# A hybrid decoder trunk with 32 experts: first-block picks with the slot matrix stationary, 8 KB of DMA scratch and an eleventh weight slot

## The chip, the cores and the metric

The kernel runs on one core of a Trainium2 chip. The metric is the device time of one execution in microseconds (us); lower is better. TensorE (PE; its weight loads are listed apart, as PEld), VectorE (DVE), ScalarE (ACT), GpSimd (POOL) and SyncE (SP) are the engines. SP issues the loads of weights; ACT issues a few transfers on a queue of its own, and POOL issues software DMAs, the indirect gathers among them.

## What is computed

One layer over 512 tokens of width 1024: a mixer of four branches with gates and an output projection `w_out`, then a mixture of experts. All is float32. The part that the change touches begins at `w_out`:

```python
x = x + g1 * hybrid_mixer(h, ..., w_out)             # ... merged @ w_out
h = rms_norm(x, norm2_g) * (1.0 + sc2) + sh2
x = x + g2 * hier_moe(h, ...)
# hier_moe, per token: top 1 of 4 groups, top 2 of its 8 experts, gate = group prob * softmax of the two
# expert e, on the tokens routed to it:
y = (silu(xe @ w1[e]) * (xe @ w3[e])) @ w2[e]        # w1, w3: 1024 x 512, w2: 512 x 1024
out = segment_sum(y * gate)
```

## The kernel before

The mixer (up to about 740 us) is the same in both kernels. After it come three stages.

**`w_out`, in two halves.** The 512 tokens are four tiles of 128; half 0 has tiles 0 and 1, half 1 has tiles 2 and 3. Each half makes four products of 256 columns (`mm<-wh,mh` and the like: 48 matmuls of three high and low terms). A result is scaled into one of two buffers `yo` by VectorE, added to `xm`, squared on ScalarE, transposed (`z`), evacuated as `xT` by ScalarE, and multiplied by the router's weights (`pl`, the logits). Half 1 uses the two weight blocks that half 0 used last, then loads and splits (`wh` on ScalarE, `wl` on VectorE) the first two again.

**Routing** (`route`, once for each half). The rows of the half, divided by their norm, are written to the DRAM tensor `xhd`: tile `t` is scaled by ScalarE into a buffer and sent by ScalarE's queue. In both halves the first tile goes through `xg[0]` (1024 columns), the second through the two `yo` buffers (512 columns each). VectorE works through a long chain of small operations (first maxima `f0`, `f1`, `f2`, one-hot rows `oe` and `ohb`); TensorE counts with `ohb` into `pl`, which gives each token's slot `rank` at its expert; `orr` is the one-hot matrix of slots. `tb` and `tg` are products with it that give each slot its token (`toki`, `tok`) and gate (`gx`, `ga`).

**Experts, two at a time.** Block `p` (0 to 15) holds experts 2p and 2p+1 with 64 slots each. `turn_in(p)` transposes the gathered rows `xg[p % 2]` and scales them to `xe`; `front` multiplies by `w1` and `w3` (`ph`, tile `g`); `Back` transposes `g`, multiplies by `w2` (`py`) and spreads the result over the tokens (`po`). The rows come from `fetch(p)`, an indirect DMA from `xhd`. Block 0 isn't fetched: its rows are picked out of `xm` by products with the first slots' one-hot matrix `rp` (in `g1b`), with `xm` as the stationary operand, eight column groups `d` by four token tiles. That gives the transposed rows at once, in `pt0`. The picks for tiles 0 and 1 stand between the routing's steps (`meanwhile`), those for tiles 2 and 3 behind `rank`. `fetch(1)` and `fetch(2)` are issued ahead of the loop, `fetch(p + 2)` in `turn_in(p)`.

**The ring of weights.** `order` lists 198 loads (186 of 1 MB, 12 of 0.5 MB), in the order in which the blocks use them. SP issues them in that order, each into the next slot of a ring of 20: `EWX` slots of the pool `ewx`, six of the freed weight pool `wst`, and four that held `mh` and `ml`, put in at the places `RL`. A load waits until its slot is free. The first `EWX` loads are issued inside half 1 of `w_out`.

TensorE's instructions run in the order of the code from here on (`manual_schedule`), VectorE's too while half 1 is routed; ScalarE's and POOL's order is the scheduler's.

Of the kernel before, what the change touches and what calls it, by code (L numbers as in the profile page):

```python
# [9 lines left out]
F32 = mybir.dt.float32  # L10
# [5 lines left out]
AF = mybir.ActivationFunctionType  # L16
# [5 lines left out]
D = 1024  # L22
KD = D // 128
NT = S // 128
# [1 line left out]
O_CV, O_SB, O_RT = 2048, 3072, 4608  # L26
TAPS = (0, 0, 1, 3, 2)
W = dict(h0=15, h1=3, h2=8, l0=7, l1=4, f0=15, sk=11, sq=7, s1=2, s2=5, s3=1, s4=5, s5=0.5, s6=3, t0=4, c0=8, c1=6, c2=9, r=5, ce=20)
EWX = 10
RL = (10, 11, 18, 19)  # L30
WS = (10, 3, 6, 6, 12)
LATE = 4
WARM = (1, 0, 0, 2)
# [4 lines left out]
def trunk(ctx, tc, x, c, ada_w, ada_b, norm1_g, norm2_g, w_in, hgrn_lb, hgrn_norm_g, conv_w, conv_b, conv_ln_g,  # L38
          conv_ln_b, sb_qnorm_g, sb_knorm_g, ret_norm_g, w_branch, w_gate, b_gate, w_out, router_group_w,
          router_group_b, router_expert_w, router_expert_b, expert_w1, expert_w3, expert_w2, out):  # L40
    nc = tc.nc
    V, A, P, T = nc.vector, nc.scalar, nc.gpsimd, nc.tensor
# [14 lines left out]
    def mm(o, l, r, start, stop):  # L57
        T.matmul(o, l, r, start=start, stop=stop, skip_group_check=True)  # L58
# [12 lines left out]
    def psm(nm="mm"):  # L71
        return ps_mm.tile([128, 512], F32, name=nm, tag="mm")

    def psz(nm="z2"):
        return ps_z.tile([128, 2, 512], F32, name=nm, tag="z2")
# [194 lines left out]
    a = A.activation(wh[:, 4:], raw[:, 4:], AF.Copy)  # L270
# [85 lines left out]
    def three(o, l, r, nk, first=True, last=True):  # L356

        (lh, ll), (rh, rl) = l, r
        for k in range(nk):
            pace()  # L360
            mm(o, lh(k), rh(k), first and k == 0, False)
            mm(o, lh(k), rl(k), False, False)
            mm(o, ll(k), rh(k), False, last and k == nk - 1)
# [597 lines left out]
    xm = keep.tile([128, NT, D], F32, name="xm")  # L961
# [44 lines left out]
    nr = nrm.enter_context(tc.tile_pool(name="nr", bufs=1))  # L1006
    yo = [nr.tile([128, 2, 256], F32, name="yo", bufs=2) for _ in range(2)]
# [26 lines left out]
    xg = [kp.tile([128, D], F32, name="xg0")]  # L1034
# [14 lines left out]

    ewx = ctx.enter_context(tc.tile_pool(name="ewx", bufs=EWX, side="right"))  # L1050
    order = []
# [14 lines left out]
    for p in range(16):  # L1066
# [5 lines left out]
        for ks, cs in cuts(p):  # L1072
            for e in es:
                order.append(four(expert_w2[0][e])[:, ks, cs])
    ring = [(ewx, "ew")] * EWX + [(wst, tag) for tag in ("raw", "raw", "wh", "wh", "wl", "wl")]
    for r, tag in zip(RL, ("ml", "mh", "ml", "mh")):
        ring[r:r] = [(late, tag)]
# [16 lines left out]
    def first_max(v, n, nm, hot=True):  # L1094

        iob = io[:, None, :n].to_broadcast([128, 2, n])
        bc = lambda a: a[:, :, None].to_broadcast([128, 2, n])
        mx = nr.tile([128, 2], F32, name=nm + "m", bufs=2)
        V.reduce_max(mx, v, axis=AX.X)
        tmp = nr.tile([128, 2, n], F32, name=nm + "t", bufs=2)  # L1100
        V.tensor_tensor(tmp, v, bc(mx), op=OP.is_lt)
        V.scalar_tensor_tensor(tmp, tmp, 64.0, iob, op0=OP.mult, op1=OP.add)
        idx = nr.tile([128, 2], F32, name=nm + "i", bufs=2)
        V.tensor_reduce(idx, tmp, axis=AX.X, op=OP.min)
        oh = None
        if hot:
            oh = nr.tile([128, 2, n], F32, name=nm + "o", bufs=2)
            V.tensor_tensor(oh, iob, bc(idx), op=OP.is_equal)
        return mx, idx, oh

    def pick(ts, ds):

        for d in ds:
            a, k = divmod(d, 4)
            for t in ts:
                mm(pt0[:, d], xm[:, t, a * 512 + k:(a + 1) * 512:4], rp[t // 2][:, t % 2], t == 0 and k == 0, t == NT - 1)

    def meanwhile():


        scr = psm("scr")
        for n, ds in zip(WARM, ((), range(4), range(4, 8), ())):
            for _ in range(n):
                mm(scr, ident, xm[:, 0, :512], True, True)
            pick((0, 1), ds)
            a = yield
            if a is not None:
                mm(scr[:a.shape[-1], :2], a, ident[:, :2], True, True)
        yield

    def fetch(p):

        P.indirect_dma_start(out=xg[p % 2], out_offset=None, in_=xhd[:, :],  # L1133
                             in_offset=bass.IndirectOffsetOnAxis(ap=toki[:, p:p + 1], axis=0),
                             bounds_check=S - 1, oob_is_err=False)
# [3 lines left out]
    oR, ev, gv, cr, rp, pt0 = [], [], [], [], [], None  # L1139

    def route(half, pl, between=None):

        then = between or (lambda a: None)
        ts = slice(2 * half, 2 * half + 2)
# [6 lines left out]
            V.scalar_tensor_tensor(lg[:, i], pl[:, i * 36:(i + 1) * 36], r[:, i:i + 1], crow, op0=OP.mult, op1=OP.add)  # L1151
        for i in range(2):
            t = 2 * half + i
            for cs, xs in ((slice(0, D), xg[0]),) if not i else ((slice(0, 512), yo[0]), (slice(512, D), yo[1])):
                if i:
                    xs = xs.rearrange("p a b -> p (a b)")
                A.activation(xs, xm[:, t, cs], AF.Copy, scale=r[:, i:i + 1])
                nc.scalar.dma_start(xhd[t * 128:(t + 1) * 128, cs], xs)
        gm, gi, og = first_max(lg[:, :, :4], 4, "f0")
# [13 lines left out]
        v2, i2, _ = first_max(eg, 8, "f2", False)  # L1173
# [10 lines left out]
        for i in range(2):  # L1184
            t = 2 * half + i
# [17 lines left out]
        if half:  # L1203
            tb = psm("tb")
            by_slot(tb[:, :16], lambda h, k_, i, j: ev[h][:, k_, i, j::2])
            slots0(1)
            pick((2, 3), range(8))
            V.tensor_scalar(toki, tb[:, :16], 1024.0, None, op0=OP.add)
            V.tensor_scalar(tok, tb[:, :16], 1024.0, None, op0=OP.add)

# [35 lines left out]
    def by_slot(o, what, first=True):  # L1246

        n = 0
        for h in range(2):
            for k_ in range(2):  # L1250
                for i in range(2):
                    for j in range(2):
                        mm(o[64 * j:64 * j + 64], oR[h][:, k_, i], what(h, k_, i, j), first and n == 0, n == 7)
                    n += 1
# [18 lines left out]
    for half in range(2):  # L1273
        pl = ps_o.tile([128, 512], F32, name="pl", tag="o1")
        ts = slice(2 * half, 2 * half + 2)
        cbs = (0, 1, 2, 3) if half == 0 else (2, 3, 0, 1)
        for n, cb in enumerate(cbs):
            if half == 0 or cb < 2:
                wo[cb] = wblock(w_out, 0, KD, cb * 256, 256)
            w = wo[cb]  # L1280
            if half and n == 3:
                load_to(EWX)
            cs = slice(cb * 256, cb * 256 + 256)
            o = psm()
            for i in range(2):
                three(o[:, i * 256:(i + 1) * 256],
                      tuple((lambda k, a=a: a[:, k, i * 128:(i + 1) * 128]) for a in (mh[half], ml[half])),
                      tuple((lambda k, a=a: a[:, k, :]) for a in w), KD, first=i == 0)
            y = yo[n % 2]
            V.tensor_mul(y, o.rearrange("p (t c) -> p t c", t=2), g1b[:, None, cs].to_broadcast([128, 2, 256]))  # L1290
            (V if half else P).tensor_add(xm[:, ts, cs], xm[:, ts, cs], y)
            for i in range(2):
                A.activation(y[:, i], xm[:, 2 * half + i, cs], AF.Square,
                             accum_out=sq2[:, 2 * half + i, cb:cb + 1])
            if n:
                logits(half, pl, n - 1, cbs[n - 1])
        between = None
        if half:
            pt0 = psz("xT").rearrange("p a (b c) -> p (a b) c", c=128)
            pe_order.enter_context(tc.manual_schedule(engines={mybir.EngineType.PE}))  # L1300
            between = meanwhile()
        logits(half, pl, 3, cbs[3], between)
        if half:
            with tc.manual_schedule(engines={mybir.EngineType.DVE}):
                slots0(0)
                next(between)
                route(half, pl, between.send)
        else:
            route(half, pl)
# [36 lines left out]
    xg.append(moe.tile([128, D], F32, name="xg1", bufs=1))  # L1346
    P.memset(xg[1], 0.0)
    fetch(1)
    fetch(2)
    ew = stream()  # L1350

    def turn_in(p):

        pt = psz("xT").rearrange("p a (b c) -> p (a b) c", c=128) if p else pt0
        for d in range(KD) if p else ():
            a, k = divmod(d, 4)
            T.transpose(pt[:, d], xg[p % 2][:, a * 512 + k:(a + 1) * 512:4], ident)  # L1357
        if 0 < p < 14:
            fetch(p + 2)
        yield  # L1360
        xe = moe.tile([128, KD, 128], F32, name="xe", bufs=1)
        for d in range(KD):
            if d % 2 and not p:
                V.tensor_scalar(xe[:, d], pt[:, d], a2s[:, d:d + 1], sh2s[:, d:d + 1], op0=OP.mult, op1=OP.add)
            else:
                A.activation(xe[:, d], pt[:, d], AF.Identity, scale=a2s[:, d:d + 1], bias=sh2s[:, d:d + 1])
        yield xe
# [149 lines left out]
    b, xe = None, list(turn_in(0))[1]  # L1517
    for p in range(16):
# [10 lines left out]
        late_, b = b, Back(p, g)  # L1529
# [6 lines left out]
        xe = next(nxt, None)  # L1536
# [33 lines left out]
```

## Time and profile before

| | us |
|---|---|
| time, median of 3 runs (1299.15 to 1299.30) | 1299.22 |
| profiled execution, its own time | 1303.05 |
| its span, first to last instruction | 1301.3 |
| PE busy | 1235.8 (95%) |
| DVE busy | 674.9 (52%) |
| ACT busy | 483.3 (37%) |
| bytes moved by DMA | 299.04 MB, mean 230 GB/s |
| mean granted TensorE clock | 0.987 of full speed |

The profile comes from one execution; its times are in us from the span's start. A busy engine is one that has an instruction under way, also when that instruction is slowed by its operands. In a timeline, a row gives the start, the time until the last of the group ends, the engine (ACTq and SPq are the issues of DMAs), the line, and in brackets how long the engine was idle before and who ended it.

### The profile page before, as it was taken

Reading aid. Unit: us, or ns where it says so; the run is one execution under the profiler, and the core shown is the slowest. Engines: PE = TensorE matmul, PEld = TensorE weight load, DVE = VectorE, ACT = ScalarE, POOL = GpSimd, SP = SyncE. Lnnn points to the kernel's source line nnn. Section 1 sums busy time; section 2 is a strip of 40 time slices with the busy share of each in tenths; the row PEclk is TensorE's granted clock in tenths of the full one; section 3 lists DMA queues with packets and bytes.
Section 4 is the critical chain, followed back from the end, with each engine's and each line's share of the span. In section 5 each row is a group of like instructions: output and inputs, shape, how many; then the busy total and the mean of one; then the engine's idle time right before and its main releaser. Section 6 shows DMA issues by size and latency. Waiting matters only on the chain.

```text
span 1301.3 us, 17173 instructions
## 1 busy us (share of the span) xinstructions
PE 1235.8 (95%) x6856; PEld 867.8 (67%) x6856; DVE 674.9 (52%) x1053; ACT 483.3 (37%) x727; POOL 209.9 (16%) x170
## 2 busy tenths in 40 slices
PE   7999998999999999998999997989999999899997
PEld 5789897987779987787888897634334433333334
DVE  2724679998964564458865444325333423232224
ACT  3447565446554465453434442112111211111110
POOL 3225846201110111122211110000000000000000
PEclk9999998999999999999999998999999999999999
DMA  9432211131222322236875297699999999999995
GB/s 328 147 112 66 97 48 52 33 97 65 88 75 65 98 65 86 77 102 202 260 223 188 88 390 259 242 420 418 419 420 419 419 419 420 419 419 420 419 413 197
DMA packets 108624, 299.04 MB, mean 230 GB/s; under 512 B 9646, under 2 KB 65054, under 8 KB 84732
## 3 DMA queue, kind: packets, MB, share of 16 engines
q1 hardware_dynamic: 102312, 289.45, 58.6%
q10 hardware_dynamic: 3588, 4.36, 1.0%
q0 software_dynamic: 2640, 4.09, 0.9%
q8 instruction: 55, 0.90, 0.3%
q14 instruction: 29, 0.24, 0.1%
HBM read 297.56 MB, written 4.20 MB: 232 GB/s over the span
## 4 chain that ended last, share of the span: by engine, by line
PE 59%; DMA 26%; DVE 5%; ACT 4%; POOL 2%; issue 2%; ACTq 0%; SPq 0%; POOLq 0%; DVEq 0%
PE mm L58 39%; DMA ew<-in_expert_w_dram 24%; PE ph L58 6%; PE py L58 3%; PE z L58 2%; PE po L58 1%; PE xT L58 1%; PE sbe L58 1%; DVE wl L254 1%; DMA adaw<-in_ada_w_dram 1%; POOL sf L577 1%; DMA xhd<-yo 1%; ACT wh L253 1%; PE sbz L58 1%; POOL hgf L578 1%
## 5 line engine op out<-in xcount | busy, mean ns | idle before, releaser
L58 PE MATMUL ph<-ew,xe 128*64 128x512 f32 x1024 | 233.1, 594 | 18.7 <-DMA ew<-in_expert_w_dram 17.9
L58 PEld LDWEIGHTS ph<-ew,xe 128*64 128x64 f32 x1024 | 77.0, 137 | 171.5 <-issue 128.9
L58 PE MATMUL mm<-hh,wh 128*128 128x512 f32 x448 | 178.9, 399 | 0.0
L58 PE MATMUL mm<-hh,wl 128*128 128x512 f32 x448 | 174.9, 390 | 1.6 <-DVE wl L266 1.6
L254 DVE TENSOR_TENSOR wl<-raw,wh 128x2048 fp32r<-128x2048 f32 x55 | 131.8, 2396 | 83.7 <-ACT wh L253 83.7
L58 PE MATMUL mm<-hl,wh 128*128 128x512 f32 x448 | 174.8, 390 | 0.0
L1434 DVE TENSOR_TENSOR xm<-xm,po 128x512 f32<-128x512 f32 (+1 forms) x136 | 81.8, 648 | 170.0 <-PE po L58 169.8
L58 PE MATMUL mm<-wh,hh 128*128 128x256 f32 x448 | 131.4, 293 | 0.0
L253 ACT ACTIVATE wh<-raw 128x2048 fp32r<-128x2048 f32 x55 | 105.1, 1911 | 69.7 <-PE mm L58 69.5
L58 PE MATMUL mm<-wl,hh 128*128 128x256 f32 x448 | 128.4, 287 | 0.0
L58 PE MATMUL mm<-wh,hl 128*128 128x256 f32 x448 | 128.2, 286 | 0.0
L58 PE MATMUL py<-ew,gT 128*64 128x512 f32 (+1 forms) x544 | 113.9, 570 | 1.3 <-ACT gT L1401 1.3
L58 PEld LDWEIGHTS mm<-hh,wh 128*128 128x128 f32 x448 | 84.2, 188 | 23.3 <-issue 7.2
L58 PEld LDWEIGHTS mm<-hh,wl 128*128 128x128 f32 x448 | 84.1, 188 | 19.9 <-DVE wl L266 1.9
L58 PEld LDWEIGHTS mm<-hl,wh 128*128 128x128 f32 x448 | 84.2, 188 | 16.5 <-DVE hl L206 0.3
L58 PEld LDWEIGHTS mm<-wh,hh 128*128 128x128 f32 x448 | 87.5, 195 | 6.0 <-issue 5.8
L58 PEld LDWEIGHTS mm<-wl,hh 128*128 128x128 f32 x448 | 87.7, 196 | 0.2
L58 PEld LDWEIGHTS mm<-wh,hl 128*128 128x128 f32 x448 | 87.5, 195 | 0.0
L58 PEld LDWEIGHTS py<-ew,gT 128*64 128x64 f32 x544 | 37.5, 137 | 69.1 <-issue 64.8
L1380 ACT ACTIVATE g<-ph 128x512 f32<-128x512 f32 x16 | 9.6, 598 | 190.6 <-PE ph L58 190.6
L1133 POOL DMA_INDIRECT xg<-xhd,toki x15 | 15.1, 1004 | 396.5 <-PE xT L1357 341.9
L157 ACT ACTIVATE yh<-py 128x512 fp32r<-128x512 f32 (+1 forms) x34 | 19.4, 572 | 140.4 <-DVE py L1422 135.2
(441 smaller groups left out, 2075.2 us busy)
## 6 DMA issues: line engine op xcount, KB each, us to landing
ew<-in_expert_w_dram SPq DMA_DIRECT2D x186, 1024.0 KB, 19.9
raw<-in_w_in_dram SPq DMA_DIRECT2D x26, 1024.0 KB, 5.0
raw<-in_w_gate_dram SPq DMA_DIRECT2D x16, 1024.0 KB, 5.5
adaw<-in_ada_w_dram SPq DMA_DIRECT2D x64, 256.0 KB, 3.3
aw<-in_ada_w_dram SPq DMA_DIRECT2D x32, 256.0 KB, 5.4
raw<-in_w_branch_dram SPq DMA_DIRECT2D x8, 1024.0 KB, 5.6
raw<-in_w_out_dram SPq DMA_DIRECT2D x6, 1024.0 KB, 5.9
ew<-in_expert_w_dram SPq DMA_DIRECT2D x12, 512.0 KB, 12.2
```

What stands on the lines that cost most here:

```text
L58: T.matmul(o, l, r, start=start, stop=stop, skip_group_check=True)
L157: A.activation(h_ap, src, AF.Copy)
L253: a = A.activation(wh, raw, AF.Copy)
L254: v = V.tensor_sub(wl, raw, wh.bitcast(F32))
L577: P.tensor_add(vw(sf)[:, :, 0], vw(sf)[:, :, 0], tb(1))
L578: P.tensor_add(vw(f)[:, :, 1], vw(f)[:, :, 1], tb(0))
L1133: P.indirect_dma_start(out=xg[p % 2], out_offset=None, in_=xhd[:, :], in_offset=bass.IndirectOffsetOnAxis(ap=toki[:, p:p + 1], axis=0), bo ...
L1380: A.activation(g, ph[:, 0], AF.Sigmoid)
L1434: V.tensor_add(xm[:, t, cs], xm[:, t, cs], po)
```

## The change

- `pick` makes the slot matrix `rp` the stationary operand and sends 512 columns of `xm` through it. The result is block 0's rows, not transposed, in two banks of PSUM (`xe`). ScalarE and VectorE copy one bank each to `xg[0]`, and `turn_in(0)` transposes and scales them as every other block's.
- `fetch(2)` moves into `turn_in(0)`, behind its transposes.
- In half 0 both tiles are scaled into `xg[0]`, one after the other, and each is sent whole. In half 1 the first tile goes through the two `yo`, the second through two buffers `xT`.
- The scratch for the descriptors of software DMAs is 8192 bytes for each partition, in place of the default of 16384. The pool `ewx` gets an eleventh slot of 8 KB, so the ring has 21, and `RL` moves by one.

```diff
-EWX = 10
-RL = (10, 11, 18, 19)
+EWX = 11
+RL = (11, 12, 19, 20)
...
-    def pick(ts, ds):
+    def pick(ts, cols=(0, 1)):
 
-        for d in ds:
-            a, k = divmod(d, 4)
+        for c in cols:
             for t in ts:
-                mm(pt0[:, d], xm[:, t, a * 512 + k:(a + 1) * 512:4], rp[t // 2][:, t % 2], t == 0 and k == 0, t == NT - 1)
+                mm(pt0[:, c], rp[t // 2][:, t % 2], xm[:, t, c * 512:c * 512 + 512], t == 0, t == NT - 1)
...
-        for n, ds in zip(WARM, ((), range(4), range(4, 8), ())):
+        for n, cs in zip(WARM, ((), (0,), (1,), ())):
...
-            for cs, xs in ((slice(0, D), xg[0]),) if not i else ((slice(0, 512), yo[0]), (slice(512, D), yo[1])):
-                if i:
-                    xs = xs.rearrange("p a b -> p (a b)")
+            parts_ = (xg[0],)
+            if half:
+                parts_ = [nr.tile([128, 512], F32, name="xT", bufs=2) for _ in range(2)] if i else [a.rearrange("p a b -> p (a b)") for a in yo]
+            for n, xs in enumerate(parts_):
+                n_ = D // len(parts_)
+                cs = slice(n * n_, n * n_ + n_)
                 A.activation(xs, xm[:, t, cs], AF.Copy, scale=r[:, i:i + 1])
                 nc.scalar.dma_start(xhd[t * 128:(t + 1) * 128, cs], xs)
...
-            pick((2, 3), range(8))
+            pick((2, 3))
+            A.activation(xg[0][:, :512], pt0[:, 0], AF.Copy)
+            V.tensor_copy(xg[0][:, 512:], pt0[:, 1])
...
-    fetch(2)
...
-        pt = psz("xT").rearrange("p a (b c) -> p (a b) c", c=128) if p else pt0
-        for d in range(KD) if p else ():
+        pt = psz("xT").rearrange("p a (b c) -> p (a b) c", c=128)
+        for d in range(KD):
...
-        if 0 < p < 14:
+        if p < 14:
             fetch(p + 2)
...
-    nc = bacc.Bacc("TRN2", target_bir_lowering=False, num_devices=1)
+    nc = bacc.Bacc("TRN2", target_bir_lowering=False, num_devices=1, dynamic_dma_scratch_size=8192)
```

Three engines get another order. ScalarE, at the end of half 0, before: the three scaled copies (L1157) and their writes to `xhd` follow each other, then comes the first split (`wh`) of half 1.

```order
L1157 ACTIVATE xg_5967<-xm,rr 128x1024
L1157 ACTIVATE yo<-xm,rr 128x512
L1158 DMA xhd<-xg_5967 128x1024
L1158 DMA xhd<-yo 128x512
L1157 ACTIVATE yo<-xm,rr 128x512
L1163 ACTIVATE ge<-ge 128x8
L1214 ACTIVATE dv<-dv 128x2
L1158 DMA xhd<-yo 128x512
L253 ACTIVATE wh<-raw 128x2048
L1293 ACTIVATE yo,sq_5981<-xm 128x256 x2
L253 ACTIVATE wh<-raw 128x2048
L1263 ACTIVATE xT<-z_6459 128x512
```

The same place after the change (line numbers there are some 2 to 4 higher):

```order
L1159 ACTIVATE xg_5967<-xm,rr 128x1024
L1165 ACTIVATE ge<-ge 128x8
L1160 DMA xhd<-xg_5967 128x1024
L1218 ACTIVATE dv<-dv 128x2
L253 ACTIVATE wh<-raw 128x2048
L1159 ACTIVATE xg_5967<-xm,rr 128x1024
L1297 ACTIVATE yo,sq_5981<-xm 128x256
L1160 DMA xhd<-xg_5967 128x1024
L1297 ACTIVATE yo,sq_5981<-xm 128x256
L253 ACTIVATE wh<-raw 128x2048
L1297 ACTIVATE yo,sq_5981<-xm 128x256 x2
L1267 ACTIVATE xT<-z_6457 128x512
```

The second scaled copy now writes the buffer that the first write still reads; one split has moved ahead of it, and four squares, the second split and the evacuation `xT` stand behind it.

VectorE, at the end of the routing of half 1, as one piece of the difference: `toki` and the gates' chain are here, and `gx` at its end feeds TensorE's products `tg`.

```order
-L1208 TENSOR_SCALAR toki<-tb 128x16
-L1209 TENSOR_SCALAR tok<-tb 128x16
-L1211 TENSOR_REDUCE gs<-ge 128x2
-L1213 TENSOR_TENSOR dv<-f2m,f1m 128x2
-L1215 SCALAR_TENSOR_TENSOR gs<-dv,gs 128x2
+L1211 COPY xg_5967<-xe 128x512
+L1212 TENSOR_SCALAR toki<-tb 128x16
+L1213 TENSOR_SCALAR tok<-tb 128x16
+L1215 TENSOR_REDUCE gs<-ge 128x2
+L1217 TENSOR_TENSOR dv<-f2m,f1m 128x2
+L1219 SCALAR_TENSOR_TENSOR gs<-dv,gs 128x2
```

The copy of the second bank has come in ahead of them. It reads what the last pick writes, and it waits for ScalarE's copy into the same tile.

POOL, at the gathers, before (`xg_5967` is `xg[0]`, `xg_6845` is `xg[1]`): `fetch(2)`, the clearing of `xg[1]`, then `fetch(1)` and `fetch(3)`.

```order
L1133 DMA xg_5967<-xhd,toki 128x1024
L1347 MEMSET xg_6845 128x1024
L1133 DMA xg_6845<-xhd,toki 128x1024 x2
L1133 DMA xg_5967<-xhd,toki 128x1024
```

After (`xg_6827` is `xg[1]`):

```order
L1351 MEMSET xg_6827 128x1024
L1132 DMA xg_5967<-xhd,toki 128x1024
L1132 DMA xg_6827<-xhd,toki 128x1024 x2
L1132 DMA xg_5967<-xhd,toki 128x1024
```

The clearing has moved ahead of `fetch(2)`, which now waits for the transposes of block 0 as well, and `fetch(1)` is still behind it.

## Rows read from the trace of the kernel before

**Rows 1.** Windows: stretch, length, busy of PE/PEld/DVE/ACT/POOL (instructions), clock, DMA share, GB/s.

```profile
780.00:790.00 10.00, 5.39 (x44) 5.22 (x44) 3.30 (x15) 1.55 (x5) 0.00 (x0) 0.92 0.93 375
790.00:800.00 10.00, 8.60 (x59) 8.30 (x58) 5.63 (x5) 3.32 (x8) 0.00 (x0) 0.73 0.62 212
...
830.00:840.00 10.00, 9.19 (x72) 4.63 (x73) 3.16 (x9) 3.11 (x5) 1.97 (x2) 1.00 0.26 64
...
839.00:1274.00 435.00, 413.64 (x1890) 168.56 (x1886) 140.82 (x276) 77.70 (x180) 12.88 (x13) 1.00 1.01 417
```

**Rows 2.** Timeline of SP's queue: issues of expert weight loads.

```profile
784.21 0.33 SPq L1086 DMA_DIRECT2D ew<-in_expert_w_dram  x1
...
807.37 1.93 SPq L1086 DMA_DIRECT2D ew<-in_expert_w_dram  x4
...
837.43 0.81 SPq L1086 DMA_DIRECT2D ew<-in_expert_w_dram  x2
```

**Rows 3.** Chain that ended last: start, us, what.

```profile
772.00 0.91 ACT yo L1293 x4
...
776.41 11.27 DMA xhd<-yo
...
1098.00 22.09 DMA ew<-in_expert_w_dram
```

**Rows 4.** Timeline of DVE, 787 to 827 us.

```profile
787.77 0.69 DVE L1290 TENSOR_TENSOR yo<-mm,g1b 128x512 f32<-128x512 f32 x1 [6.63 <-DMA xhd<-yo]
...
822.00 0.29 DVE L1195 TENSOR_TENSOR oo<-oe,pl 128x128 f32<-128x128 f16 x1 [4.94 <-PE pl L58]
...
824.25 0.17 DVE L1208 TENSOR_SCALAR toki<-tb 128x16 int32<-128x16 f32 x1
...
826.17 0.49 DVE L1227 TENSOR_TENSOR gx<-oe,gh 128x128 f16<-128x128 f16 x2
```

**Rows 5.** Timeline of PE, 789 to 848 us.

```profile
789.29 1.09 PE L1260 MATMUL z<-ident,xm 128*128 128x128 f32 x4 [4.61 <-issue]
...
791.99 0.58 PE L58 MATMUL mm<-wl,mh 128*128 128x256 f32 x1 [1.40 <-DVE wl L254]
...
815.76 4.00 PE L58 MATMUL xT<-g1b,xm 128*128 128x128 f32 x16
819.82 1.98 PE L58 MATMUL scr<-xm,ident 128*128 128x512 f32 x4
...
824.39 7.74 PE L58 MATMUL xT<-g1b,xm 128*128 128x128 f32 x32 [0.96 <-DVE g1b L1243]
832.05 0.68 PE L58 MATMUL tg<-gx,orr 128*64 128x16 f16 x32
...
834.61 13.10 PE L58 MATMUL ph<-ew,xe 128*64 128x512 f32 x60 [0.20 <-DVE xe L1364]
```

**Rows 6.** Timeline of ACT, 775 to 781 us.

```profile
775.79 0.36 ACTq L1158 DMA_DIRECT2D xhd<-xg  x1
...
778.86 1.92 ACT L253 ACTIVATE wh<-raw 128x2048 fp32r<-128x2048 f32 x1 [0.23 <-PE mm L58]
```

**Rows 7.** Groups by line and shape, 750 to 860 us: busy us, mean ns.

```profile
L1366 ACT ACTIVATE xe<-xT,mod 128x128 f32<-128x128 f32 x12 | 4.9, 466 | 10.8 <-PE tg L58 8.0 <-DVE xe L1364 2.3 <-PE xT L1357 0.5
...
L1263 ACT ACTIVATE xT<-z 128x512 f32<-128x512 f32 x8 | 4.7, 589 | 20.9 <-PE z L1260 20.9
...
L1157 ACT ACTIVATE xg<-xm,rr 128x1024 f32<-128x1024 f32 x2 | 2.3, 1153 | 1.6 <-DVE rr L148 1.6
...
L1357 PE MATMUL xT<-ident,xg 128*128 128x128 f32 x8 | 1.2, 297 | 0.0
```

**Rows 8.** Timeline of POOL: the gathers.

```profile
834.15 1.01 POOL L1133 DMA_INDIRECT xg<-xhd,toki  x1 [0.27 <-POOL xg L1347]
...
930.61 0.99 POOL L1133 DMA_INDIRECT xg<-xhd,toki  x1 [25.59 <-PE xT L1357]
```

**Rows 9.** Waits of SP's queue, 740 to 860 us: total, times, longest.

```profile
SPq L1086 <- DMA xhd<-xg: 22.5, 2, 12.0
```

More of the change, by code (lines that the diff above doesn't have):

```diff
@@ L1109, in first_max @@
         return mx, idx, oh
-    def pick(ts, ds):
-        for d in ds:
-            a, k = divmod(d, 4)
+    def pick(ts, cols=(0, 1)):
+        for c in cols:
             for t in ts:
-                mm(pt0[:, d], xm[:, t, a * 512 + k:(a + 1) * 512:4], rp[t // 2][:, t % 2], t == 0 and k == 0, t == NT - 1)
+                mm(pt0[:, c], rp[t // 2][:, t % 2], xm[:, t, c * 512:c * 512 + 512], t == 0, t == NT - 1)
     def meanwhile():
         scr = psm("scr")
-        for n, ds in zip(WARM, ((), range(4), range(4, 8), ())):
+        for n, cs in zip(WARM, ((), (0,), (1,), ())):
             for _ in range(n):
                 mm(scr, ident, xm[:, 0, :512], True, True)
-            pick((0, 1), ds)
+            pick((0, 1), cs)
             a = yield
@@ L1298, in trunk @@
         if half:
-            pt0 = psz("xT").rearrange("p a (b c) -> p (a b) c", c=128)
+            pt0 = psz("xe")
             pe_order.enter_context(tc.manual_schedule(engines={mybir.EngineType.PE}))
```

## The prediction

> **What bounds the kernel now.** I read the windows by stage first. From 839 to 1274 us the DMA engines are full (share 1.01, 417 GB/s) at full TensorE clock, while between 780 and 840 the share falls to 0.62 and even 0.26 [rows 1]. The expert stage is therefore a stream of 1 MB weight loads, and it ends as late as it does because it stood still before 839. TensorE is not its bound: a gather, which follows each block's transposes, comes 25.59 + 0.99 = 26.6 us after the one before it [rows 8], and a block's twelve loads of 1.05 MB take 30.2 us at 417 GB/s.
>
> Next, the loads' issue times say what held the stream. The load that restarted it went out at 837.43, when the first expert product let go of slots 0 and 1 [rows 2]. All 20 slots had been filled from 807.37 on, when the last `w_out` product ended. So each us by which TensorE reaches the first expert product earlier, and each MB more that fits in the ring before it, takes time off the end.
>
> Third, what made TensorE late. The chain of waits holds an 11.27 us piece, the write `xhd<-yo` [rows 3]: VectorE waited 6.63 us for it, because `yo` was to be written again [rows 4], and TensorE stood 4.61 us behind that [rows 5]. After the pause the clock was 0.73 on average from 790 to 800 [rows 1], a mixture of the levels 2.4 and 1.2 GHz. In the routing VectorE waits 4.94 us for the count product `pl` [rows 4], which is queued behind two groups of picks of 4.00 us, and the last picks take 7.74 us [rows 5].
>
> **The change part by part.**
>
> *Half 0 of the normalised rows.* Both tiles now go through `xg[0]`, so half 1 writes `yo` without waiting. The wait that takes its place stands on ScalarE: the second copy into `xg[0]` needs the first write landed. That write was issued at 775.79 [rows 6], and a load that waited for it (up to 12.0 us [rows 9]) went out at 784.21 [rows 2]: a landing 8.4 us after the issue. I keep 784.2; the other write's 11.27 us [rows 3] is the bound above. Queued behind the waiting copy on ScalarE are four squares, a split and the evacuation of `xT` that TensorE's logits need: 1.15 (copy) + 2 x 0.91 (pairs of squares) + 1.92 (split) + 0.59 (evacuation) [rows 3, 6, 7] = 5.5, with hand-overs 5.8, so `xT` is there at 790.0. The first split of half 1 (778.86) is ahead of the waiting copy and is safe.
> TensorE ended its previous product at 789.29 - 4.61 = 784.7 [rows 5]; with four transposes (half of 1.09, which was at half clock) and a short wait for the routing's one-hot rows it starts the third product at 785.6. From 791.99 [rows 5] to 807.37 [rows 2] this and the fourth product needed 15.4. The mean clock of 0.73 from 790 to 800 is 5.4 us at half clock, of which 2.0 lie ahead of 791.99; the other 3.4 cost 1.7, so the work is 13.7 at full clock. The third product reaches its logits after 24 matmuls of 5.39/44 = 0.12 us [rows 1], at 788.5, and stands there for 1.5 us. The end: 785.6 + 13.7 + 1.5 = 800.8. **Gain 807.4 - 800.8 = 6.6 us.** A landing earlier than 782.7 gives 1.5 more; each us later takes one away.
>
> *Picks with the slot matrix stationary.* No row shows this product; the nearest is a 128x512 float32 product of `ident`, of which two take 1.98 [rows 5] (as four records). Each early group becomes two such products: 2 x (4.00 - 1.98) = 4.0, less than VectorE's 4.94 us of waiting, so all of it is on the path. The late group becomes four: 7.74 - 3.96 = 3.8. The bounds: at the present picks' 0.25 us a record the groups would take 1.0, 1.0 and 2.0 (4.9 gained early, by VectorE's wait, and 5.7 late); at half clock they would take as long as now. I take the row of 512 columns at full clock, as it is the same shape.
>
> *Copies and transposes.* They are new on the path. ScalarE's copy counts 0.59 [rows 7]; VectorE's, which by the order waits for ScalarE, 0.7 (the 128x512 row of 0.69 [rows 4]). `toki`, gates and `gx` stand behind it on VectorE, 824.25 to 826.66 = 2.4 us [rows 4]; they lay under the picks before and don't any more, and TensorE's products `tg` wait for them. Then three quarters of `tg`'s 0.68 [rows 5], eight transposes 1.2 and one `xe` 0.47 [rows 7]: 5.9 in all, where before 834.61 - 832.13 = 2.5 [rows 5] lay between the last pick and the steady expert product. That is 3.4 lost. The first of sixteen steps of the expert product (13.10/15 = 0.87) was hidden before and is not now. **Picks and copies together: 4.0 + 3.8 - 3.4 - 0.9 = 3.5 us gained.**
>
> *The clock.* The copies open a pause of about 4 us ahead of the expert product, which started at full clock until now. The pause of 4.61 us was followed by half clock [rows 1, 5]. One such stretch at the start of the product, as long as the 3.4 us above, costs half its length. I take **1.7 us lost**, between nothing and 3.4 (two stretches). The Trainium skill (TensorE: Matmul & The Clock Gate, "HAM oscillation — how this bites in real kernels") speaks against this part too: waits between groups of products bring the low clock back again and again. The row of the pause agrees; without that rule and that row the sum below would be 1.7 better.
>
> *One more slot.* Eleven loads instead of ten can be out before the half ends, and 21 instead of 20 before the restart: 1.05 MB less to load after it, at 417 GB/s [rows 1] **2.5 us gained**. The gap is long enough for it (share 0.26 in 830 to 840).
>
> *The gathers and the scratch.* The gather for block 2 moves behind the transposes of block 0, and on POOL it is ahead of that for block 1, which so goes out a gather's issue, 1.0 us, later after the same point; 834.15 before [rows 8], about 831 less the 6.6 now. It is wanted when the first expert product ends, 13 us on. The moved gather's bytes (at most 128 rows of 4 KB, 1.3 us) now fall into the full stretch: 0 to 1.3, **0.7 lost**, as not every slot is filled. Half the scratch may make POOL wait until an earlier gather has landed; the trace shows no such wait. I count nothing. With a wait of 11.27 (the longest written row [rows 3]) and as much again to land, TensorE would stand some 10 us ahead of block 1, while the eight slots that block 0 has freed by then are 20 us of loads: nothing on the end either. The Trainium skill (SBUF — State Buffer, "SBUF size: 192, 224, or 256?") names 16 KB as the carve-out for these descriptors, so this kernel runs with half of it; no run here shows what that does.
>
> *Sum:* 6.6 + 3.5 - 1.7 + 2.5 - 0.7 = 10.2. It is taken from the profiled execution (1303.05 us, span 1301.3) and carried over to the median, which is 0.3% less: 1299.2 - 10.2 = **1289.0 us**.
>
> **The rivals.**
> *The wait moves to ScalarE and eats half 1's gain.* For it: the write is served beside a saturated stream, and another one took 11.27. If it lands 15.0 us after its issue, the first term is nothing: 3.6 gained, 1295.6. Against it: 8.4 measured for the same write in the same place.
> *Only the slot counts.* If the stream's restart hung on something else than TensorE, what is left is 2.5 - 0.7 = 1.8: 1297.4, no change to be told. For it: the queue of loads does wait for landings, up to 12.0 us [rows 9]. Against: the load at 837.43 [rows 2] went out just as three more steps of 0.87 after 834.61 [rows 5] had let go of the first two slots.
> *Slower.* The same ScalarE wait, as long as the longest weight load in the chain, 22.09 [rows 3]: `xg[0]`'s write lands at 798, the first term becomes 6.6 - 13.8 = -7.2 and the sum -3.6: 1302.8. It decides from a landing at 797 on, 21 us after the issue. Against: no written row took over 11.3.
>
> **How the numbers follow.** Forecast 0.76 (its own range 1285.1 to 1295.3: down to it: no clock loss, no stand of TensorE for `xT` and a free gather, 1.7 + 1.5 + 0.7; up to it: a landing of 11.27, 2.9, and two more stretches at half clock, 3.4), moved wait 0.12, slot alone 0.07, slower 0.05. A measurement of this kernel tells about 0.2%, 2.6 us, from no change. The forecast and most of the moved wait are faster by more than that: 0.86; within it: 0.09; slower: 0.05. Leaving out the slot alone, the slower case and the far ends of the forecast gives 1285.5 to 1296.
>
> **What would show it.** After the change: no wait of VectorE on an `xhd` write; ScalarE idle before the second `xg` copy until about 784; the last `w_out` product's end near 801; VectorE's wait for `pl` near 1 us in place of 4.94; picks of some 2, 2 and 4 us; the first reload near 829 (837.43 - 6.6 - 3.5 + 1.7) and a full stretch from there to the end. The forecast is wrong if the first write lands after 790, if the picks keep their length, or if the DMA share drops again after the restart.

## The result and the profile after

The changed kernel takes 1291.24 us (median of 4 runs, 1290.93 to 1292.99) where the kernel before took 1299.26 beside it: a ratio of 0.9929 (95% interval 0.9908 to 0.995). It is faster by 8.0 us; 10.2 were forecast, and 1291.2 lies inside the range.

The two profiled executions differ by more, 12.2 us in their spans, and not all of that is the change's. Two points that both kernels have tell how much: the start of half 0's last `yo` product on VectorE, which lies ahead of every edit, and TensorE's last product. Two rows before, then two after, from the timelines of VectorE and TensorE:

```profile
769.93 0.69 DVE L1290 TENSOR_TENSOR yo<-mm,g1b 128x512 f32<-128x512 f32 x1 [6.57 <-PE mm L58]
```

```profile
1293.31 0.28 PE L58 MATMUL po<-yl,pT 128*128 128x256 f32 x1
```

```profile
767.51 0.69 DVE L1294 TENSOR_TENSOR yo<-mm,g1b 128x512 f32<-128x512 f32 x1 [6.53 <-PE mm L58]
```

```profile
1280.11 0.28 PE L58 MATMUL po<-yl,pT 128*128 128x256 f32 x1
```

The execution after was 2.4 us ahead when it came to the first changed instruction. From there to the last product it took 512.6 in place of 523.4, **10.8 us less**, and behind the last product 1.0 more (1289.1 - 1280.1 = 9.0 in place of 8.0). 2.4 + 10.8 - 1.0 = 12.2. This length between the two points is used below, as it leaves the start of the program out: the second profile of the old order (e4 below) has 523.7, though it came to the first point 3.3 us sooner.

The windows after (columns as in [rows 1]):

```profile
780.00:790.00 10.00, 8.39 (x72) 8.19 (x72) 5.93 (x11) 5.14 (x11) 0.00 (x0) 1.00 1.02 421
790.00:800.00 10.00, 9.25 (x79) 8.83 (x78) 3.35 (x6) 2.32 (x7) 0.00 (x0) 1.00 0.75 295
810.00:817.00 7.00, 4.20 (x24) 1.85 (x25) 2.27 (x9) 0.80 (x2) 0.00 (x0) 1.00 0.93 341
817.00:824.00 7.00, 4.93 (x38) 3.06 (x39) 4.15 (x17) 1.37 (x3) 3.06 (x3) 0.51 0.12 30
824.00:828.00 4.00, 4.00 (x20) 1.26 (x18) 0.47 (x2) 1.74 (x2) 0.00 (x0) 1.00 0.52 124
828.00:1262.00 434.00, 416.55 (x1894) 169.74 (x1891) 140.91 (x277) 78.44 (x181) 12.91 (x13) 0.99 1.01 417
```

Against [rows 1]: the stretch at a clock of 0.73 between 790 and 800 is gone, and a new one at 0.51, all but wholly 1.2 GHz, stands from 817 to 824. The full stretch of the DMA engines now begins at 828. Two more stretches at 0.51 lie inside it, the first of them here:

```profile
840.90:844.40 3.50, 3.33 (x8) 1.00 (x10) 0.00 (x0) 0.46 (x2) 0.00 (x0) 0.51 1.02 418
```

The timelines of SP, ScalarE, VectorE, TensorE and POOL after:

```profile
798.25 1.28 SPq L1086 DMA_DIRECT2D ew<-in_expert_w_dram  x3
...
826.50 3.76 SPq L1086 DMA_DIRECT2D ew<-in_expert_w_dram  x3
```

```profile
773.37 0.36 ACTq L1160 DMA_DIRECT2D xhd<-xg  x1
...
781.84 1.16 ACT L1159 ACTIVATE xg<-xm,rr 128x1024 f32<-128x1024 f32 x1 [3.61 <-DMA xhd<-xg]
```

```profile
776.42 0.69 DVE L1294 TENSOR_TENSOR yo<-mm,g1b 128x512 f32<-128x512 f32 x1
...
808.86 0.29 DVE L1197 TENSOR_TENSOR oo<-oe,pl 128x128 f32<-128x128 f16 x1 [0.92 <-PE pl L58]
...
815.61 0.69 DVE L1211 COPY xg<-xe 128x512 f32<-128x512 f32 x1 [4.42 <-ACT xg L1210]
816.21 0.17 DVE L1212 TENSOR_SCALAR toki<-tb 128x16 int32<-128x16 f32 x1
...
818.14 0.49 DVE L1231 TENSOR_TENSOR gx<-oe,gh 128x128 f16<-128x128 f16 x2
```

```profile
787.08 1.08 PE L58 MATMUL pl<-wr,xT 128*128 128x36 f32 x8 [1.61 <-ACT xT L1267]
...
811.24 3.70 PE L58 MATMUL xe<-xm,g1b 128*128 128x512 f32 x8 [0.96 <-DVE g1b L1247]
...
818.47 0.81 PE L58 MATMUL tg<-gx,orr 128*64 128x16 f16 x24 [3.31 <-DVE gx L1231]
819.22 1.98 PE L1360 MATMUL xT<-ident,xg 128*128 128x128 f32 x8
```

```profile
821.49 1.09 POOL L1132 DMA_INDIRECT xg<-xhd,toki  x1 [1.05 <-PE xT L1360]
```

VectorE's 6.63 us for an `xhd` write [rows 4] are gone; ScalarE waits 3.61 for the first write, which landed 781.84 - 773.37 = 8.5 us after its issue, and TensorE stands 1.61 behind that. VectorE's wait for `pl` fell from 4.94 [rows 4] to 0.92, the last picks from 7.74 [rows 5] to 3.70. New are VectorE's 4.42 ahead of its copy, with `toki` to `gx` behind, and TensorE's 3.31 for `gx`.

### The profile page after: what moved, and what is told of

It is laid out like the page before. It is cut to its first block, busy times and chain, and to the rows that moved or that the text cites. A ratio compares the mean times of both kernels' runs of the same rounds, so it can differ in the third digit from the quotient of the medians.

```text
span 1289.1 us, 17096 instructions
## 1 busy us (share of the span) xinstructions
PE 1226.0 (95%) x6816; PEld 851.6 (66%) x6816; DVE 675.3 (52%) x1054; ACT 484.1 (38%) x728; POOL 210.2 (16%) x170
## 5 line engine op out<-in xcount | busy, mean ns | idle before, releaser
L58 PE MATMUL ph<-ew,xe 128*64 128x512 f32 x1024 | 234.0, 600 | 14.6 <-DMA ew<-in_expert_w_dram 13.9
```

## The experiments

The table cuts the length into four pieces that the SP and TensorE timelines give: from the first point (half 0's last `yo` product) to the first pick, over the picks, from the last pick's end to the load that restarts the stream, and from there to the last product. "End" is what follows the start of the last product. Each kernel has one profile; the pieces that an edit does not touch differ by up to 0.5 among them. The ratio is that of the runs' times to the kernel before, run on the same chip.

| kernel | ratio (95% interval) | to picks | picks | to restart | to last product | length | end |
|---|---|---|---|---|---|---|---|
| before | 1 | 41.8 | 20.4 | 5.3 | 455.9 | 523.4 | 8.0 |
| after | 0.9929 (0.9908-0.995) | 35.1 | 12.3 | 11.6 | 453.6 | 512.6 | 9.0 |
| e1 ten slots | 0.9948 (0.993-0.9966) | 34.8 | 12.3 | 11.6 | 456.0 | 514.8 | 9.4 |
| e2 rows alone | 0.9947 (0.9926-0.9968) | 35.0 | 20.4 | 5.3 | 456.0 | 516.7 | 8.4 |
| e3 slot matrix alone | 0.9997 (0.9984-1.0009) | 41.7 | 12.3 | 10.9 | 455.9 | 520.8 | 9.3 |
| e4 scratch alone | 0.9995 (0.9984-1.0007) | 42.0 | 20.4 | 5.3 | 456.0 | 523.7 | 7.9 |
| e5 own buffer, ten slots | 0.9933 (0.9906-0.996) | 34.1 | 13.9 | 10.8 | 456.0 | 514.9 | 9.3 |
| e6 copies late | 0.988 (0.9852-0.9908) | 35.2 | 12.3 | 6.4 | 453.5 | 507.5 | 7.1 |
| e7 filler | 0.9896 (0.9873-0.9919) | 34.9 | 12.3 | 11.1 | 453.2 | 511.6 | 7.2 |
| e8 first write from SP | 0.9922 (0.9894-0.9949) | 33.6 | 12.3 | 11.8 | 453.3 | 510.9 | 8.0 |
| e9 e6 and e8 | 0.989 (0.9871-0.9909) | 33.5 | 14.0 | 6.4 | 453.5 | 507.5 | 8.2 |
| e10 second write | 0.9973 (0.9956-0.9991) | 41.3 | 12.3 | 11.8 | 453.6 | 519.1 | 7.5 |
| e11 e9 and one product | 0.9879 (0.9859-0.9899) | 33.6 | 12.3 | 6.4 | 453.7 | 506.1 | 8.0 |

The four parts of the change were run apart first.

**e1, ten slots.** The changed kernel with the ring before:

```diff
-EWX = 11
-RL = (11, 12, 19, 20)
+EWX = 10
+RL = (10, 11, 18, 19)
```

> The changed kernel with ten and twenty slots as before; the scratch stays at 8 KB. Theory (four terms that add up: rows 6.6, picks and copies with the clock 1.8, slot 2.5, the moved gather -0.7): the restart of the stream stays where the changed kernel has it, 28 to 29 us behind the last w_out product's end, and the time is 2.5 above the changed kernel, 1293.7. Rival A (the slot carries the gain): 1297 or more. Rival B (the stream does not need the place, since its loads are late for another reason): within 0.5 of 1291.2.

The length is 514.8, 2.2 above the changed kernel; the ratio is 0.9948, some 6.8 us below the kernel before. The first three pieces are the same to 0.3, the fourth is 456.0 in place of 453.6. So the slot is worth 2.4 behind the restart. Rival A falls by the times as well; rival B falls by the length alone, as the intervals of the two ratios overlap.

**e2, the rows of half 0 alone.**

```diff
-            for cs, xs in ((slice(0, D), xg[0]),) if not i else ((slice(0, 512), yo[0]), (slice(512, D), yo[1])):
-                if i:
+            for cs, xs in ((slice(0, D), xg[0]),) if not (half and i) else ((slice(0, 512), yo[0]), (slice(512, D), yo[1])):
+                if half and i:
```

> The kernel before, with the one edit that both tiles of half 0 are written through xg[0]; picks, gathers, slots and scratch as before. Theory: VectorE's wait for an xhd write is gone, ScalarE waits for the first write instead, the last w_out product ends 6.6 us earlier than in the kernel before, and the whole gain arrives at the end: 1299.3 - 6.6 = 1292.7. Rival A (only the slot counts): 1299. Rival B (the wait moves and eats a part): between 1294 and 1299, with TensorE standing more than 3 us for the evacuation of xT on ScalarE.

The waits of 780 to 800 (columns: total, times, longest) no longer hold an `xhd<-yo`:

```profile
ACT xg L1157 <- DMA xhd<-xg: 3.5, 1, 3.5
...
PE pl L58 <- ACT xT L1263: 1.5, 1, 1.5
```

The first piece is 6.8 shorter, the others unchanged, the length 6.7 less, and the ratio, some 6.9 us, says the same. The rows alone bring what was forecast for them. "Only the slot counts" is refuted, and so is a wait that eats a part beyond the 1.5 already counted.

**e3, the slot matrix alone.** The picks, copies, transposes and the moved gather of the change in the kernel before, with ten slots and 16 KB; half 0 writes as before (`elif half or i` keeps `yo` there). The edit against the changed kernel, without the slots and the scratch:

```diff
-            if half:
-                parts_ = [nr.tile([128, 512], F32, name="xT", bufs=2) for _ in range(2)] if i else [a.rearrange("p a b -> p (a b)") for a in yo]
+            if half and i:
+                parts_ = [nr.tile([128, 512], F32, name="xT", bufs=2) for _ in range(2)]
+            elif half or i:
+                parts_ = [a.rearrange("p a b -> p (a b)") for a in yo]
```

> The kernel before, with the slot matrix stationary in the picks, the copies and transposes that follow, and the moved gather; the half 0 rows go through yo as before, ten slots, 16 KB of scratch. (Half 1 has the two tiles that the changed kernel uses, since xg[0] takes the copies.) Theory: picks and copies 3.5 less the clock 1.7 less the gather 0.7, so 1.1 gained: 1298.2. Rival A (the copies, the longer chain and the half clock give back all of it): 1299.3 or above. Rival B (the whole 3.5 arrive): 1295.8.

The picks take 12.3 in place of 20.4, so 8.1 less; 5.6 of it are given back between the last pick and the restart. What remains is 2.5 in the length, between the theory's 1.1 and rival B's 3.5. The fourth piece is that of before (455.9 both), so the moved gather costs nothing there. The times see only 0.4 of the gain, with an interval from 2.1 faster to 1.2 slower, and so they don't rule out rival A: the part behind the last product took 1.4 more in this profile (9.35 in place of 7.95), which would leave 1.1.

**e4, the scratch alone.**

```diff
-    nc = bacc.Bacc("TRN2", target_bir_lowering=False, num_devices=1)
+    nc = bacc.Bacc("TRN2", target_bir_lowering=False, num_devices=1, dynamic_dma_scratch_size=8192)
```

> The kernel before with 8 KB of scratch for the software DMAs in place of 16, and nothing else changed. Theory: no gather waits for the landing of an earlier one longer than the stream hides, so 1299.3 within 0.5, and POOL's issues keep their 0.99 us. Rival (the smaller scratch holds up POOL and takes back a part of the changed kernel's gain): slower by 1 to 3 us, with longer issues or with gaps ahead of them on POOL. Its profile is besides a second one of the program before: if it is some 4 us shorter than the one shown, the profiled execution of before was a long one, and 12.2 us between the two profiles is not all the change's.

No change: 0.9995. The gathers keep their time; POOL's group of them, in this run:

```profile
L1133 POOL DMA_INDIRECT xg<-xhd,toki x15 | 15.1, 1004 | 397.0 <-PE xT L1357 342.0 <-DVE gx L1227 54.7 <-POOL xg L1347 0.3
```

All that POOL waited for is TensorE, VectorE and itself, never a landing. The 16 KB that the Trainium skill (SBUF — State Buffer, "SBUF size: 192, 224, or 256?") names for these descriptors are not needed by these fifteen gathers, which for the most part follow each other at 26.6 us [rows 8].

The second group looks for what the new waits cost.

**e5, half 0's second tile in a buffer of its own,** with ten slots, and so to be read beside e1.

```diff
+            if not half and i:
+                parts_ = (nr.tile([128, D], F32, name="xq", bufs=1),)
```

> The changed kernel with ten and twenty slots, and half 0's second tile in a buffer of its own, so that ScalarE's second copy waits for no landing. To be read beside the changed kernel with ten slots, whose length from half 0's last yo product to TensorE's last product is 514.8. Theory: ScalarE's 3.4 us of idle time and TensorE's 1.6 for xT go, the last w_out product ends 1.5 earlier and the length is 513.3. Rival (half 1 is held by something else at that place, the split of wh or VectorE's sums): 514.8 within 0.3, with TensorE's wait only under another name.

Beside e1: ScalarE's and TensorE's waits for the landing are gone (TensorE's was 1.35 there; one of 0.20 for `wl` is new), the picks start 0.7 sooner, not 1.5, and nothing arrives: the length is the rival's. Where it went stands in TensorE's timeline and in the windows:

```profile
809.83 5.33 PE L58 MATMUL xe<-xm,g1b 128*128 128x512 f32 x8 [0.96 <-DVE g1b L1249]
```

```profile
809.70:813.10 3.40, 3.27 (x4) 1.50 (x5) 0.07 (x1) 0.00 (x0) 0.00 (x0) 0.50 0.95 325
```

A stretch at 1.2 GHz fell on the last picks: 5.33 for what takes 3.70 at 2.4 GHz. The stretch behind the picks is shorter for it, 820.0 to 823.4 where e1 has 6.8 us of half clock, and gives back 0.8. So 0.7 of the wait was on the path, and the clock took its gain; why it was 0.7 and not more is not shown.

**e6, the copies behind `gx`.**

```diff
             pick((2, 3))
-            A.activation(xg[0][:, :512], pt0[:, 0], AF.Copy)
-            V.tensor_copy(xg[0][:, 512:], pt0[:, 1])
             V.tensor_scalar(toki, tb[:, :16], 1024.0, None, op0=OP.add)
...
         gv.append(gx)
         if half:
+            A.activation(xg[0][:, :512], pt0[:, 0], AF.Copy)
+            V.tensor_copy(xg[0][:, 512:], pt0[:, 1])
             tg = psm("tg")
```

> The changed kernel with the two copies out of the picks' accumulator written behind gx, so that toki, the gates and gx run on VectorE while TensorE picks. Changed kernel: length 512.6 from half 0's last yo product to TensorE's last product, 28.3 from the last w_out product's end to the restart. Theory: the chain of 2.4 and the product tg leave the path, the transposes start 3.0 earlier; with the pause cut from 3.5 to about 0.5 the clock stays at 2.4 GHz, worth 0.8 in the transposes and 1.1 in the first expert product: 4.9 in all, restart 23.4 behind the last w_out product, length 507.7. Rival A (the half clock comes all the same): 3.0, restart 25.3, length 509.6. Rival B (the time to the restart is not passed on to the end, because the ring is full later): length 511 or more with the restart moved.

Length 507.5: the theory's 4.9 came as 5.1, all of it between last pick and restart. The timeline of VectorE and TensorE, and one window:

```profile
816.17 0.48 DVE L1229 TENSOR_TENSOR gx<-oe,gh 128x128 f16<-128x128 f16 x2
818.01 0.68 PE L58 MATMUL tg<-gx,orr 128*64 128x16 f16 x32
...
818.77 1.47 PE L1360 MATMUL xT<-ident,xg 128*128 128x128 f32 x8
```

```profile
780.00:845.00 65.00, 57.81 (x385) 36.27 (x385) 27.06 (x91) 21.14 (x47) 4.04 (x4) 1.00 0.90 355
```

`gx` is there 1.4 us before the last pick ends, `tg` waits for nothing, the transposes follow at once, and the clock stays at 2.4 GHz; the trace grants the full clock through to 1270.

**e7, filler in the pause.**

```diff
             pick((2, 3))
+            sc = psm("scr")
+            for _ in range(3):
+                mm(sc, ident, xm[:, 0, :512], True, True)
```

> The changed kernel with three 128x512 products of ident (3.0 us) behind the last pick, into the scratch accumulator: TensorE works through most of the pause of 3.5 us, and nothing waits for them that would not have waited for gx. Theory (the pause brings the half clock): 1.00 granted from 815 to 828, eight transposes in 1.1 instead of 1.93, the first expert product 1.1 shorter, restart and length 1.9 earlier, 510.7. Rival A (the slow start is not the clock's, but the alternation of ScalarE and VectorE over xe): the transposes get shorter, the expert product does not, 0.8. Rival B (the clock falls because of the copies' waits that are still there, about 0.5 us): no change, 512.6.

Half right. The pause ahead of `tg` shrinks from 3.31 to 0.74, but the clock falls once all the same, only later and for half as long:

```profile
818.00:820.20 2.20, 1.71 (x32) 1.49 (x31) 1.66 (x6) 0.40 (x1) 1.15 (x2) 1.00 0.04 7
820.20:823.60 3.40, 3.29 (x8) 1.00 (x10) 1.72 (x6) 1.94 (x5) 1.90 (x2) 0.50 0.41 96
```

The transposes are shorter (1.23 in place of 1.98) and the first expert product is not (15.56 in place of 14.97). The length is 1.0 less, but only 0.4 of that lies between the last pick and the restart, where the filler stands; the other 0.6 is in pieces that it doesn't touch. Filling one pause did not prevent the fall; waits of 0.74 and 0.60 remained behind the filler.

**e8, the first write from SP.** Only the first tile's write was moved, not both as the expectation says:

```diff
-                nc.scalar.dma_start(xhd[t * 128:(t + 1) * 128, cs], xs)
+                (nc.scalar if t else nc.sync).dma_start(xhd[t * 128:(t + 1) * 128, cs], xs)
```

> The changed kernel, with the two xhd writes of half 0 issued by SP behind the weight loads instead of by ScalarE, so that the first lands later: its landing is what this run moves. Theory: each us by which ScalarE's second copy starts later moves the last w_out product's end and the restart by one us. With a landing 12 us after the issue in place of 8.5 the length is 516, with 22 us 526. Rival (ScalarE's work is not on the path): 512.6 whatever the landing. If the write lands in the same 8.5, the run tells nothing on this.

The landing came earlier, not later, so this tests the theory from the other side. SP waited for ScalarE's copy before it issued, the loads behind it stood too, and the DMA engines were idle for 4 us; the write then went out at the head of an empty queue, ahead of those loads. Windows, and ScalarE's timeline:

```profile
770.00:774.00 4.00, 4.00 (x35) 3.85 (x34) 2.56 (x16) 2.58 (x8) 0.00 (x0) 1.00 0.01 4
```

```profile
778.13 1.14 ACT L1159 ACTIVATE xg<-xm,rr 128x1024 f32<-128x1024 f32 x1
```

Issued at 773.36, it had landed before 778.13, under 4.8 us, and ScalarE did not wait. The picks start 1.5 earlier, as the prediction had it for a landing before 782.7, and the length is 1.65 less, so the rival falls. The 4 us without loads cost nothing: the ring is full before the restart either way.

**e10, a second write of the same tile,** into a DRAM tile of its own on ScalarE's queue.

```diff
                 nc.scalar.dma_start(xhd[t * 128:(t + 1) * 128, cs], xs)
+                if not t:
+                    nc.scalar.dma_start(xh2, xs)
```

> The changed kernel, with half 0's first tile written a second time by ScalarE's queue, into a DRAM tile that nobody reads: 512 KB more that have to land before ScalarE may write xg[0] again. In the changed kernel the write's packets ran from 776.9 to 781.0 beside the stream, 8.46 us after the issue. Theory: the second write takes 4 us more, ScalarE's second copy starts 12.5 after the issue, TensorE stands 5.6 instead of 1.6, and the last w_out product, the restart and the end come 4.0 later: length 516.6; with half clock behind a stand as long as the 4.61 of the kernel before up to 518.3. Rival (the copy's lateness is made good in the routing, where VectorE and TensorE wait for each other): less than 2 of it arrive, 514.6 or less.

The timelines of ScalarE and TensorE:

```profile
788.45 1.15 ACT L1160 ACTIVATE xg<-xm,rr 128x1024 f32<-128x1024 f32 x1 [7.64 <-DMA xh<-xg]
```

```profile
793.64 1.92 PE L58 MATMUL pl<-wr,xT 128*128 128x36 f32 x8 [5.38 <-ACT xT L1270]
```

Both landed 12.5 after the first's issue at 775.95, TensorE stood 5.38, and the half clock that the change had removed was back, granted 0.50 from 792.2 to 799.0. The length is 519.1: 6.5 more for a landing 4.0 later, where the theory gave 4.0, or up to 5.7 with the half clock. The rival falls; the price of a late landing is higher than an us for an us, as the stand brings the clock down too.

**e9, e6 and e8 together,** and **e11,** the same with one product in TensorE's wait ahead of the last picks:

```diff
             slots0(1)
+            mm(psm("scr"), ident, xm[:, 0, :512], True, True)
             pick((2, 3))
```

> The copies behind gx and half 0's first xhd write from SP, together. By themselves they shortened the length from half 0's last yo product to TensorE's last product by 5.1 and 1.65 against the changed kernel's 512.6. Theory (both move TensorE's way to the first expert product, at two places, so they add): 505.8, the restart 52.7 behind the yo product, and no half clock between 780 and 1270. Rival A (the stream's pause of 4 us that SP's wait makes counts now, since TensorE is there sooner and the ring is not full in time): 507.5. Rival B (the half clock comes back by where the pauses fall): 507.5 to 508.

> The kernel with the copies late and the first xhd write from SP, with one 128x512 product of ident (0.99 us) in TensorE's wait of 0.96 us ahead of the last picks, where the half clock of 3.4 us fell in the run without it (last picks 5.40 in place of 3.70, and 1.6 of the gain gone). Theory (that wait and the one of 0.70 ahead of it bring the fall, and the fall alone ate the gain): 1.00 granted from 780 to 1270, last picks 3.70, length from half 0's last yo product to TensorE's last product 505.8 to 505.9. Rival A (the fall comes at another place in the routing): 507 to 508. Rival B (the last picks are not on the path to the restart): 507.5 with 1.00 granted.

e9 gained nothing over e6, as its rival B has it: its picks start 1.65 sooner and last 1.7 longer, with 0.51 granted from 813.6 to 817.0. TensorE's timeline in e9:

```profile
813.45 5.40 PE L58 MATMUL xe<-xm,g1b 128*128 128x512 f32 x8 [0.96 <-DVE g1b L1247]
```

In e11 the wait is filled; TensorE's timeline and the window:

```profile
811.78 1.12 PE L58 MATMUL scr<-xm,ident 128*128 128x512 f32 x2
812.81 3.70 PE L58 MATMUL xe<-xm,g1b 128*128 128x512 f32 x8
```

```profile
780.00:837.00 57.00, 52.92 (x360) 34.57 (x358) 27.08 (x91) 20.39 (x46) 4.05 (x4) 1.00 1.00 398
```

The picks are back at 3.70 and the length is 506.1, against 505.8 to 505.9 expected: the fall had eaten the gain. The full clock does not last to 1270 as expected: 0.57 is granted from 837 to 841, but that lies behind the restart at 823.0 and cost nothing. This is the shortest of all, 1284.6 us by its median (ratio 0.9879), though the times alone don't tell it from e6.

## Why the prediction came out as it did

The forecast was right in its mechanism and in most of its terms; the pieces of the table stand for the steps.

- *Half 0 of the rows, 6.6:* measured 6.7 (41.8 to 35.1), and 6.8 alone. The landing after 8.5 (8.4 forecast) and TensorE's stand of 1.61 (1.5) are as worked out.
- *Picks, 4.0 + 3.8 = 7.8:* measured 8.1, at the price of the `ident` product. The bound at 0.25 us a record was not it.
- *Copies and transposes, 3.4 + 0.9, and the clock, 1.7, together 6.0 given back:* measured 6.3 (5.3 to 11.6). The half clock lasted from 817 to 824, twice the stretch that was taken, but its first 1.4 us lay on TensorE's wait for `gx`. The single terms were not measured apart at full clock. Where the half clock there lasted 6.8 us the piece is 11.6 to 11.8 (after, e1, e8, e10), where it lasted 3.4 it is 10.8 to 10.9 (e3, e5), so the longer one costs 0.8 more, half of the 1.7 that the prediction took for each 3.4; e6 shows that with the chain off the path and no half clock only 1.1 of the 6.3 is left. The rule of the Trainium skill (TensorE: Matmul & The Clock Gate, "HAM oscillation — how this bites in real kernels"), that waits between groups of products bring the low clock back, agrees with the waits of 3.31 us here and 5.38 us in e10. It does not tell e5 and e9 from e1 and e6: the same waits of 0.70 and 0.96 us stand ahead of the last picks in all four, and 0.50 and 0.51 were granted on the picks of e5 and e9, 1.00 on those of e1 and e6.
- *The slot, 2.5:* 2.4. The lengths behind the restart fall into two sets, 455.9 to 456.0 in the six kernels with ten slots and 453.2 to 453.7 in the seven with eleven.
- *The moved gather, 0.7 lost:* nothing (455.9 in e3, 455.9 before). Here the prediction read the place wrongly: block 2's gather did not move into the full stretch. It went out at 821.49 and had landed at 825.0, in the pause before the restart at 826.50. *The scratch:* nothing, as counted.

The restart came 67.5 - 59.0 = 8.5 earlier where 8.4 were forecast (6.6 + 3.5 - 1.7), and the last product 10.8 where the sum was 10.2. What the prediction did not have is the part behind the last product: 9.0 in place of 8.0, and so 9.8 in the end. The medians show 8.0, the ratio with its interval 6.5 to 12.0. Between 7.1 and 9.4 us lie behind the last product in the thirteen profiles, while the products ahead of it keep their spacing and the last output store is issued 0.8 us behind it in all of them. In part it is that store's landing that differs. The DMA queues after, from 1283.0 to 1284.8, 2.9 to 4.7 us behind the last product:

```profile
q1 hardware_dynamic: 32, 0.03, 6.0%
```

These are the store's last packets; they keep about one of the 16 DMA engines busy (6.0%) and end 4.5 us behind the last product, where before the last one ended at 2.8. The four profiles with an end of 9.0 or more (after, e1, e3, e5) have such packets up to 4.4 or 4.5; in the nine others they end at 2.8, and the end still varies from 7.1 to 8.4. The changed code alone does not bring the late packets, as e7, e8 and e10 hold all of the change and don't have them. No run here was made for that, and the cause stays open.

Of the rivals, "only the slot counts" is refuted by e2. "The wait moves to ScalarE" is real, as e10 shows, and did not decide, since the write landed after 8.5. For "slower" the prediction put the point of decision at a landing 21 us after the issue, at an us lost for each us; at e10's 6.5 for 4.0 the whole gain of 10.8 would be gone some 6.7 us behind the changed kernel's 8.5, near 15 (an estimate from these two runs alone).

## What to carry to other kernels

Follow a shorter product to what stands behind it: the picks became 8.1 us shorter, and 6.3 went to copies, a chain that had lain under the picks, and the half clock that the new pause brought; putting the chain back under them (e6) kept 5.1 of that. Where TensorE has waits, moving or removing one can put the half clock on another stretch and eat the gain (e5, e9), so read the granted clock of the whole stage before a part is called worthless. And a buffer that a queued write must leave before it is used again is a wait of that write's landing, here 8.5 us beside a full stream and under 4.8 ahead of one that had stopped: it does not vanish with a change of buffer, it moves to the engine that writes next.

## What the runs showed of the hardware

The old picks hardly felt the clock. In the kernel before, 0.50 was granted from 826.0 to 829.4, inside the last group of picks, yet 32 of them took 7.74, 0.24 each, where the early ones took 0.25 at 1.00 [rows 5]. The window of before:

```profile
826.00:829.40 3.40, 3.40 (x16) 3.40 (x16) 0.62 (x4) 0.00 (x0) 1.16 (x1) 0.50 0.27 81
```

The new ones, with 512 columns moving, go from 3.70 to 5.33 with such a stretch on them (e5). So the change made the picks faster and made them depend on the clock, which the prediction had only as a bound: at half clock throughout they would take some 7.7 more (an estimate: 3.70 + 2 x 1.98 at full clock, doubled), nearly all of the 8.1.

Behind the restart TensorE's clock did not count. The changed kernel and e7 have two stretches of 3.4 us at half clock there, e6 and e9 none, and from the restart to the last product they take 453.6, 453.2, 453.5 and 453.5. The DMA engines are full in that time (1.02 in the stretch from 840.9 to 844.4).
